# A hybrid decoder layer: the Mamba branch's TensorE instructions in a written order instead of the planner's

## The chip, the cores and the metric

The kernel runs on one core of one Trainium2 chip. The metric is device time in microseconds (us), the median of several executions; smaller is better. One core has TensorE (PE; its weight loads are shown as PEld), VectorE (DVE), ScalarE (ACT), GpSimd (POOL), the sync engine's queue (SP), which issues most transfers, and 16 DMA engines.

## The reference, cut to what matters

One layer on 512 tokens of width 1024, all in f32. A projection feeds an attention branch and a Mamba-2 branch; gates merge them, then come an output projection, a LayerNorm, a SwiGLU FFN and a second LayerNorm. The change touches the Mamba branch alone:

```
z, xbc, dt_raw = parts of x @ w_in
xbc = silu(causal_depthwise_conv(xbc, conv_w, conv_b))       # 4 taps along the tokens
xs, bm, cm = split(xbc, [2048, 2048 + 512])                  # 32 heads of 64; 4 groups of B and C, state 128
# chunks of 128 tokens, decay = exp(acum_t - acum_s) for s <= t
y_diag = (C B^T * decay) @ (x * dt)                          # within a chunk
h_next = h * exp(acum_last) + B^T @ (x * dt * decay_to_end)  # state, chunk to chunk
y = y_diag + exp(acum) * (C @ h_prev) + d_skip * xs
u = y * silu(z);  u = u * rsqrt(mean(u^2 per group) + eps) * norm_w
ssm_d = u @ w_proj_ssm
```

## The kernel before, in words

**A product.** `mm3` (L143) multiplies two operands that are each split in a rounded high part and a low rest: three matmuls (L144 to L146) of 128x128 weights by up to 512 columns. In this text one call of it is a step. Weights come by SP into `raw` tiles (4 buffers), ACT makes the high part (L102, `whi`) and DVE the low part (L103, `wlo`, 3 buffers each), both marked urgent.

**One group.** The branch has four groups `g` of eight heads. `group_bc` (L274) projects B and C of the group (8 steps each); `conv_evac` (L260) takes each result through the convolution: one ACT pass (L262), three DVE taps (L265), an ACT tanh (L268); `silu_to` (L272, DVE) ends it. B is then transposed on TensorE (four 128x128 transposes, L289), and C and B give four products (L295), which DVE masks into `cbm` (L296). `group_x` (L301) projects 256 columns of x per call (two blocks of 128, 16 steps in all), runs the same convolution on each block, transposes it (L311) and copies it to `xtok` (L312). `group_y` (L325) goes over four chunks: `xdt` (DVE, L338), two decay tiles `ab` loaded by SP from a table in HBM (L344), eight relu and two exp passes on ACT (L347, L348), two DVE products with `cbm` (L349); then TensorE makes eight products of 64 columns (L353, `py`), `C @ h_prev` (L362, `po`) and the state (L370, `pst`); POOL makes `dx` (L356) and `xw` (L368); DVE adds up `y` (L359 to L365) and the next state `hn` (L375, L376). `group_z` (L315) projects z (32 steps) and makes `gz`. `group_u` (L381) gates and normalises `y` (DVE L386, ACT L388, POOL L390, DVE L391) and transposes it (L395) into `uh` and `ul`. `group_proj` (L399) multiplies by the output weights (32 steps), and ACT or DVE adds the result to `sd` (L405, L407).

**PSUM.** There are four banks for the long products (`gps`) and four for everything short (`cps`). POOL's `xw`, `dx` have one buffer each, `xdt` two, `ab` six.

**The order.** The main loop is L647 to L666: for each group `group_y`, then the output projection of the group before, z, `group_u`, then B, C and x of the next group; at the end the q and k projections of the first heads and the last output projection. This text order is only a priority: a planner that builds the program takes, for each engine, the ready instruction of highest priority by its own estimate of time, and the result is a fixed order per engine. On the chip each engine runs its list in that order and waits where an operand is late. Where the kernel opens a manual region for an engine, the instructions of that engine stand in text order; `high_priority` marks instructions to be preferred.

The functions before the change:

Of the kernel before, what the change touches and what calls it, by code (L numbers as in the profile page):

```python
# [2 lines left out]

# [10 lines left out]
ALU = mybir.AluOpType  # L14
# [3 lines left out]
P = 128  # L18
T = 512
NT = T // P  # L20
# [6 lines left out]
NG = 4  # L27
# [14 lines left out]
def tile_hybrid_decoder_layer(  # L42
# [62 lines left out]
    def gps():  # L105
        return psum.tile([P, T], F32, name="gps", bufs=4)
# [43 lines left out]

    def gemm_ws(w, c0, nk, rhs, evac, alloc=gps, n=T, chunks=None):
# [9 lines left out]
        for b in range(2):  # L161
            evac(b, ps[b])

    def gemm_xs(w, c0, lhs, evac, before=None):


        ps = [gps() for _ in range(NT)]

# [10 lines left out]
        if before is None:  # L179
            for kc in range(KD // 2):  # L180
                hi, lo = split_w(fetch(kc), T)
                for tt in range(NT):
                    product(kc, tt, hi, lo)
            return
# [5 lines left out]
        with tc.manual_schedule(engines=ORDERED):  # L190
            for i in range(NT):
                before(i)
                for kc in range(len(chunks)):
                    product(kc, i, *chunks[kc])
                chunks.append(split_w(raw[i], T, urgent=False))
                if i == NT - 1:
                    small_weights()
                for tt in range(i + 1):
                    product(i, tt, *chunks[i])

    def down_chunk(w, kc, half, dst=None):
# [71 lines left out]

    def group_bc(g):  # L274
        st = {}
# [5 lines left out]
        for bi, nm in ((0, "bT"), (1, "cT")):  # L281
            v, th = conv_evac(16 + 4 * bi + g, gp[bi])
            st[nm] = slot(nm)
            silu_to(st[nm], v, th)
        bT, cT = st["bT"], st["cT"]
        btok = st["btok"] = slot("btok")
        ps = cps()
        for c in range(NT):
            nc.tensor.transpose(out=ps[:, c * P:(c + 1) * P], in_=bT[:, c * P:(c + 1) * P], identity=ident)  # L289
        nc.scalar.copy(out=btok, in_=ps)  # L290
        cbm = st["cbm"] = slot("cbm", (P, NT, P))
        ps = cps()
        for c in range(NT):
            cs = slice(c * P, (c + 1) * P)
            nc.tensor.matmul(out=ps[:, cs], lhsT=bT[:, cs], rhs=cT[:, cs], start=True, stop=True)  # L295
        nc.vector.tensor_tensor(out=cbm, in0=ps.rearrange("p (c l) -> p c l", c=NT),  # L296
                                in1=tri.rearrange("p (o l) -> p o l", o=1).broadcast_to([P, NT, P]), op=ALU.mult)
        st["xtok"] = big("xtok")
        return st

    def group_x(g, st, pair):  # L301
        xtok = st["xtok"]

        def evac(b, ps):
            j = 2 * pair + b
            v, th = conv_evac(4 * g + j, ps)
            xst = slot("xst")
            silu_to(xst, v, th)
            pt = cps()
            for c in range(NT):  # L310
                nc.tensor.transpose(out=pt[:, c * P:(c + 1) * P], in_=xst[:, c * P:(c + 1) * P], identity=ident)  # L311
            nc.scalar.copy(out=xtok[:, :, j * P:(j + 1) * P], in_=pt.rearrange("p (c f) -> p c f", c=NT))  # L312
        gemm_ws(w_in, C_X + g * 512 + pair * 256, KD, rhs_x, evac)

    def group_z(g, before=None):  # L315
        gz = big("gz")

        def evac(tt, ps):
            th = slot("th")
            nc.scalar.activation(out=th, in_=ps, func=AF.Tanh, scale=0.5)  # L320
            nc.vector.scalar_tensor_tensor(out=gz[:, tt, :], in0=th, scalar=1.0, in1=ps, op0=ALU.add, op1=ALU.mult)
        gemm_xs(w_in, C_Z + g * 512, lhs_x, evac, before)
        return gz

    def group_y(g, st):  # L325
        cT, btok, cbm, xtok = st["cT"], st["btok"], st["cbm"], st["xtok"]
# [5 lines left out]
        hprev = None  # L332
        ys = []
        for c in range(NT):
# [5 lines left out]
            for hf in range(2):  # L340
# [8 lines left out]
                nc.vector.tensor_tensor(out=m, in0=m, in1=cbm[:, c:c + 1, :].broadcast_to([P, 4, P]), op=ALU.mult)  # L349
                ms.append(m)  # L350
            py = cps()
# [3 lines left out]
            dx = slot("dx")  # L355
            nc.gpsimd.tensor_tensor(out=v8(dx), in0=v8(xc),  # L356
                                    in1=d_bc[:, h8].rearrange("p (h o) -> p h o", o=1).broadcast_to([P, 8, 64]), op=ALU.mult)
            y = slot("y")
            nc.vector.tensor_tensor(out=y, in0=py, in1=dx, op=ALU.add)  # L359
            if c > 0:  # L360
                po = cps()
                nc.tensor.matmul(out=po, lhsT=cT[:, cs], rhs=hprev, start=True, stop=True)  # L362
                yo = slot("yo")
                nc.vector.tensor_tensor(out=v8(yo), in0=v8(po), in1=bc8(ecum, c), op=ALU.mult)
                nc.vector.tensor_tensor(out=y, in0=y, in1=yo, op=ALU.add)  # L365
            if c < NT - 1:
                xw = slot("xw")
                nc.gpsimd.tensor_tensor(out=v8(xw), in0=v8(xc), in1=bc8(dtw, c), op=ALU.mult)  # L368
                pst = cps()
# [7 lines left out]
                hprev = hn  # L377
            ys.append(y)
        return ys

    def group_u(g, ys, gz):  # L381
        uh, ul = big("uh", 4, F32R), big("ul", 4, F32R)
        for c in range(NT):
            cs = slice(c * P, (c + 1) * P)
            y = ys[c]
# [5 lines left out]
            nc.vector.scalar_tensor_tensor(out=y, in0=y, scalar=ss[:, 1:2], in1=nw_bc[:, g * 512:(g + 1) * 512],  # L391
                                           op0=ALU.mult, op1=ALU.mult)
            pu = cps()
# [3 lines left out]
        return uh, ul  # L397

    def group_proj(g, u):  # L399
        uh, ul = u  # L400
        for pair in range(4):
            def evac(b, ps, pair=pair):
# [3 lines left out]
                else:  # L406
                    nc.vector.tensor_tensor(out=o, in0=ps, in1=o, op=ALU.add)  # L407
            gemm_ws(w_ps[g * 512:(g + 1) * 512], pair * 256, 4, lambda kt: (uh[:, kt, :], ul[:, kt, :]), evac)


    QK = (("v", "th", "bT", "cT"), ("btok", "cbm", "xst", "xdt"))

    def att_qk(hg, isq, qk):
        c0 = (C_Q if isq else C_K) + hg * 256
        sc = 0.125 if isq else 1.0

        def evac(b, ps):
            for par in range(2):
# [14 lines left out]
                qk[(isq, h)] = (t1, t2)  # L433
        gemm_ws(w_in, c0, KD, rhs_x, evac)

    def att_v(hg):
# [9 lines left out]
        gemm_xs(w_in, C_V + hg * 256, lhs_x, evac)  # L446
        return vt

# [192 lines left out]

    st = group_bc(0)
    for pair in range(2):
        group_x(0, st, pair)
    nw_bc = slot("nw", (P, 2048))
    nc.sync.dma_start(out=nw_bc, in_=ssm_norm_w.partition_broadcast(P))
    qk = {}  # L647
    u = None
    for g in range(NG):
        ys = group_y(g, st)  # L650
        if g == 0:
            st = group_bc(1)
            group_x(1, st, 0)
        else:
            group_proj(g - 1, u)
            gz = group_z(g)
        u = group_u(g, ys, gz)
        if g == 0:
            group_x(1, st, 1)
        elif g < NG - 1:  # L660
            st = group_bc(g + 1)
            for pair in range(2):
                group_x(g + 1, st, pair)
    att_qk(0, True, qk)
    att_qk(0, False, qk)
    group_proj(NG - 1, u)  # L666

# [7 lines left out]
    for hg in range(4):  # L675
        if hg > 0:
            att_qk(hg, True, qk)
            att_qk(hg, False, qk)
        if hg % 2 == 0:
            vts = att_v(hg)  # L680
        vt = vts[hg % 2]
# [413 lines left out]
```

## Time and profile before

| | us |
|---|---|
| median of 3 runs (lowest to highest) | 1146.16 (1146.07 to 1146.4) |
| profiled execution, its own time | 1149.0 |
| span of the profiled execution | 1147.3 |

The profile is of one execution, with times from the start of its span. Busy time of TensorE is a union of modelled matmul spans: a 512-column product is shown at 0.39 us though the next may start after 0.23 us. So here the starts of successive instructions are compared, not the spans. The stage that the change touches runs from about 44 to 438 us; attention, the output projection and the FFN follow.

### The profile page before, as it was taken

The numbers are of one execution on the slowest core, as the hardware profiler recorded it, in microseconds if no ns is written. First come the engines' busy times: TensorE is split into PE (matmuls) and PEld (weight loads), VectorE is DVE, ScalarE is ACT, GpSimd is POOL, SyncE is SP. The second block draws the span as 40 slices with busy tenths as digits, with TensorE's granted clock in tenths as the row PEclk, the third lists the DMA queues.
The fourth block names the chain that finished last, engine by engine and source line by source line (L and its number), as shares of the span: only waits on it lengthen the run. The fifth ranks groups of instructions, "written<-read, shape, count | busy, mean of one in ns | idle before, by whom it ended". The sixth has DMA issues, their size and how long they took to land.

```text
span 1147.3 us, 15795 instructions
## 1 busy us (share of the span) xinstructions
PE 1118.0 (97%) x6086; PEld 941.3 (82%) x6086; DVE 777.8 (68%) x1223; ACT 527.2 (46%) x912; POOL 134.1 (12%) x165
## 2 busy tenths in 40 slices
PE   7999999999999999999999999999999999999996
PEld 5887778778787788777777888888999999988885
DVE  2679974884786563889598534556997777767326
ACT  2476664454542432666465434214654554453210
POOL 3003130030122100221110000011111111100001
PEclk9999999999999999999999999999999999999998
DMA  6353233233232233211212245381778787465311
GB/s 195 110 169 127 75 112 101 82 111 101 83 94 58 89 92 96 70 57 56 77 53 56 76 127 183 108 204 59 199 184 204 183 195 164 91 231 174 102 55 74
DMA packets 116060, 134.20 MB, mean 117 GB/s; under 512 B 5669, under 2 KB 94481, under 8 KB 115857
## 3 DMA queue, kind: packets, MB, share of 16 engines
q1 hardware_dynamic: 98896, 111.75, 31.8%
q0 software_dynamic: 14640, 14.10, 7.7%
q10 hardware_dynamic: 2448, 7.34, 1.8%
q8 instruction: 48, 0.79, 0.3%
q14 instruction: 28, 0.22, 0.1%
HBM read 128.78 MB, written 4.26 MB: 116 GB/s over the span
## 4 chain that ended last, share of the span: by engine, by line
PE 44%; DVE 3%; issue 3%; DMA 2%; ACT 1%; POOL 0%; POOLq 0%; DVEq 0%; ACTq 0%
PE gps L145 9%; PE gps L144 9%; PE gps L146 9%; PE cps L145 5%; PE cps L146 5%; PE cps L144 4%; DMA rq<-in_w_ffn_up_dram 1%; PE cps L480 1%; PE cps L486 1%; DMA t_sd<-in_x_dram 0%; DVE xr L763 0%; PE cps L458 0%; DMA raw<-in_w_ffn_down_dram 0%; PE cps L459 0%; DVE wlo L103 0%
## 5 line engine op out<-in xcount | busy, mean ns | idle before, releaser
L103 DVE TENSOR_TENSOR wlo<-raw,whi 128x1024 fp32r<-128x1024 f32 x127 | 156.2, 1230 | 189.3 <-ACT whi L102 188.6
L102 ACT CAST whi<-raw 128x1024 fp32r<-128x1024 f32 x127 | 133.4, 1051 | 253.5 <-PE gps L145 101.9
L145 PE MATMUL gps<-xl,whi 128*128 128x512 f32 x456 | 181.2, 397 | 0.0
L144 PE MATMUL gps<-xh,whi 128*128 128x512 f32 x456 | 181.0, 397 | 0.0
L146 PE MATMUL gps<-xh,wlo 128*128 128x512 f32 x456 | 180.8, 396 | 0.0
L102 ACT CAST wh<-rq 128x1024 fp32r<-128x1024 f32 (+1 forms) x84 | 82.2, 980 | 101.7 <-PE cps L145 44.6
L103 DVE TENSOR_TENSOR wl<-rq,wh 128x1024 fp32r<-128x1024 f32 (+1 forms) x84 | 95.0, 1132 | 34.2 <-ACT wh L102 34.1
L144 PEld LDWEIGHTS gps<-xh,whi 128*128 128x128 f32 x456 | 85.9, 188 | 16.3 <-issue 0.2
L145 PEld LDWEIGHTS gps<-xl,whi 128*128 128x128 f32 x456 | 86.0, 189 | 16.1 <-issue 0.2
L146 PEld LDWEIGHTS gps<-xh,wlo 128*128 128x128 f32 x456 | 86.0, 189 | 15.4
L144 PE MATMUL gps<-whi,xh 128*128 128x512 f32 x192 | 76.1, 397 | 1.9 <-ACT whi L102 1.6
L145 PE MATMUL gps<-wlo,xh 128*128 128x512 f32 x192 | 75.8, 395 | 1.0 <-DVE wlo L103 1.0
L146 PE MATMUL gps<-whi,xl 128*128 128x512 f32 x192 | 75.8, 395 | 0.0
L265 DVE SCALAR_TENSOR_TENSOR t_v<-gps,cw,t_v 128x511 f32<-128x511 f32 (+2 forms) x72 | 53.4, 745 | 3.9 <-ACT t_v L262 3.1
L145 PE MATMUL gps<-t_ul,whi 128*128 128x512 f32 x128 | 51.1, 399 | 0.0
L146 PE MATMUL gps<-t_uh,wlo 128*128 128x512 f32 x128 | 51.0, 399 | 0.0
L144 PE MATMUL gps<-t_uh,whi 128*128 128x512 f32 x128 | 50.5, 394 | 0.0
L144 PEld LDWEIGHTS gps<-whi,xh 128*128 128x128 f32 x192 | 36.5, 190 | 10.7 <-ACT whi L102 2.0
L465 ACT ACTIVATE t_y<-t_y,sm 128x128 f32<-128x128 f32 (+1 forms) x64 | 35.7, 559 | 19.4 <-DVE sm L463 17.7
L347 ACT ACTIVATE t_ab<-t_ab,acum 128x128 f32<-128x128 f32 x128 | 41.6, 391 | 5.7 <-DMA t_ab<-ac_d 5.4
L821 POOL DMA_DIRECT2D rq<-in_w_ffn_gate_dram x12 | 15.5, 1294 | 245.7 <-ACT xh L723 159.0
L145 PEld LDWEIGHTS gps<-wlo,xh 128*128 128x128 f32 x192 | 36.5, 190 | 9.3 <-DVE wlo L103 1.9
(567 smaller groups left out, 2761.3 us busy)
## 6 DMA issues: line engine op xcount, KB each, us to landing
raw<-in_w_in_dram SPq DMA_DIRECT2D x80, 512.0 KB, 3.7
rq<-in_w_ffn_gate_dram SPq DMA_DIRECT2D x25, 512.0 KB, 5.8
rq<-in_w_ffn_up_dram SPq DMA_DIRECT2D x25, 512.0 KB, 5.9
raw<-in_w_ffn_down_dram SPq DMA_DIRECT2D x22, 512.0 KB, 4.0
t_ab<-ac_d SPq DMA_DIRECT2D x32, 256.0 KB, 3.3
raw<-in_w_proj_ssm_dram SPq DMA_DIRECT2D x16, 512.0 KB, 3.5
rq<-in_w_ffn_gate_dram POOLq DMA_DIRECT2D x10, 512.0 KB, 7.8
rq<-in_w_ffn_up_dram POOLq DMA_DIRECT2D x10, 512.0 KB, 6.4
```

The costliest lines, as they stand in the source:

```text
L102: nc.scalar.copy(out=hi, in_=src)
L103: nc.vector.tensor_tensor(out=lo, in0=src, in1=hi.bitcast(F32), op=ALU.subtract)
L144: nc.tensor.matmul(out=o, lhsT=l[0], rhs=r[0], start=start, stop=False, skip_group_check=skip)
L145: nc.tensor.matmul(out=o, lhsT=l[0], rhs=r[1], start=False, stop=False, skip_group_check=skip)
L146: nc.tensor.matmul(out=o, lhsT=l[1], rhs=r[0], start=False, stop=stop, skip_group_check=skip)
L265: nc.vector.scalar_tensor_tensor(out=v[:, sh:], in0=ps[:, 0:T - sh], scalar=cw[:, k, blk:blk + 1], in1=v[:, sh:], op0=ALU.mult, op1=ALU.add)
L347: nc.scalar.activation(out=m[:, r, :], in_=m[:, r, :], func=AF.Relu, scale=-1.0, bias=acum[:, c, h:h + 1])
L465: nc.scalar.activation(out=pt[:, 0:n], in_=pt[:, 0:n], func=AF.Exp, scale=-1.0, bias=sm[:, 2:3], accum_out=sm[:, 0:1])
L480: nc.tensor.transpose(out=ps[:, o:o + P], in_=pr[i][:, kb * P:(kb + 1) * P], identity=ident)
L486: nc.tensor.matmul(out=po[:, kb * P:], lhsT=vt[:, kb, hh, :], rhs=pT[kb][j], start=kb == 0 and j == 0, stop=kb == NT - 1 and j == 1)
L821: nc.gpsimd.dma_start(out=self.v(t), in_=self.q(*s_), accum_op=ALU.add)
```

## The change

For the whole branch TensorE gets a manual region: its instructions run in the order of the text. The functions become generators that yield after each step, and the main loop says how many steps stand between them. `fill(steps, n)` runs n steps; `later` holds transposes (and the C*B products) with a count of steps after which they are put in. The count is lowered right after the step that finished the source, so `[9, ...]` means 8 further steps, 8 means 7 and 10 means 9. `at(steps, ns, what)` runs the given numbers of steps and a piece of `what` after each. Results of the two blocks of one x pair are now evacuated when each block's last step is issued. The convolution, the copy to `xtok`, the whole of `y_steps` and `u_steps` are marked high priority. In a chunk of y the preparation (`xdt`, `ab`, `xw`, `dx`) is one piece and the TensorE products (`py`, `po`, `pst`) with what follows them another; `hn` comes ahead of `y`. Helpers `ws_steps`, `xs_steps`, `proj_steps` are the old loops with a yield after each `mm3`. No arithmetic, tile or transfer is added or removed. The core:

```diff
+    later = []
+
+    def fill(steps, n=10 ** 6):
+        for _ in range(n):
+            if next(steps, 0) == 0:
+                return
+            for e in later:
+                e[0] -= 1
+            while later and later[0][0] <= 0:
+                later.pop(0)[1]()
+
+    def bc_steps(g, st):
...
+                if kt == KD - 1:
+                    nm = ("bT", "cT")[bi]
+                    with tc.high_priority():
+                        v, th = conv_evac(16 + 4 * bi + g, gp[bi])
+                        st[nm] = slot(nm)
+                        silu_to(st[nm], v, th)
+                    later.append([9, (b_tok, c_b)[bi]])
+                yield 1
...
+    def x_steps(g, st, pair):
...
+            with tc.high_priority():
+                v, th = conv_evac(4 * g + j, ps)
+                xst = slot("xst")
+                silu_to(xst, v, th)
...
+            later.append([(8, 10)[b], to_tokens])
+        yield from ws_steps(w_in, C_X + g * 512 + pair * 256, KD, rhs_x, evac)
...
+    def y_steps(g, st, ys):
...
+            if c < NT - 1:
+                xw = slot("xw")
+                nc.gpsimd.tensor_tensor(out=v8(xw), in0=v8(xc), in1=bc8(dtw, c), op=ALU.mult)
+            dx = slot("dx")
...
+            yield 1
             py = cps()
...
+    def u_steps(g, ys, gz):
...
+        yield 1
+        for c in range(NT):
...
             pu = cps()
...
+            yield 1
...
+    def at(steps, ns, what):
+
+        for n in ns:
+            fill(steps, n)
+            with tc.high_priority():
+                next(what)
+
+    def bcx(g):
+        return chain(bc_steps(g, sts[g]), x_steps(g, sts[g], 0), x_steps(g, sts[g], 1))
+
+    with tc.manual_schedule(engines={mybir.EngineType.PE}):
+        fill(bcx(0))
+        nw_bc = slot("nw", (P, 2048))
+        nc.sync.dma_start(out=nw_bc, in_=ssm_norm_w.partition_broadcast(P))
+        for g in range(NG):
+            after = bcx(g + 1) if g < NG - 1 else chain(att_qk(0, True, qk), att_qk(0, False, qk))
+            ys = []
+            if g == 0:
+                fill(after, 11)
+                at(after, (0, 3, 0, 6, 0, 6, 0, 6), y_steps(g, sts[g], ys))
+                at(after, (0, 6, 3, 3, 3), u_steps(g, ys, gz))
+            else:
+                proj = proj_steps(g - 1, *u[0])
+                fill(proj, 11)
+                at(proj, (0, 4, 0, 6, 0, 6, 0, 5), y_steps(g, sts[g], ys))
+                fill(proj)
+                gz, steps = group_z(g)
+                fill(steps)
+                at(after, (0, 8, 3, 3, 3), u_steps(g, ys, gz))
+            fill(after)
+        fill(proj_steps(NG - 1, *u[0]))
```

## Rows read from the trace of the kernel before

**Rows 1.** The page, part 1: busy time of TensorE, its share, instructions.
```profile
PE 1118.0 (97%) x6086; PEld 941.3 (82%) x6086; DVE 777.8 (68%) x1223; ACT 527.2 (46%) x912; POOL 134.1 (12%) x165
```

**Rows 2.** Timeline, TensorE, ends of the stage (start us, us, instruction).
```profile
44.38 0.39 PE L144 MATMUL gps<-xh,whi 128*128 128x512 f32 x1
...
45.74 0.39 PE L144 MATMUL gps<-xh,whi 128*128 128x512 f32 x1
...
438.00 0.39 PE L144 MATMUL gps<-whi,xh 128*128 128x512 f32 x1
```

**Rows 3.** Timeline, TensorE, the u transposes of group 1.
```profile
196.57 0.39 PE L145 MATMUL gps<-xl,whi 128*128 128x512 f32 x1
...
204.21 0.63 PE L395 MATMUL cps<-ident,t_y 128*128 128x128 f32 x4 [0.73 <-DVE t_y L391]
...
204.90 0.39 PE L144 MATMUL gps<-xh,whi 128*128 128x512 f32 x1
```

**Rows 4.** Timeline, TensorE, state products of group 2.
```profile
243.63 0.40 PE L145 MATMUL gps<-t_ul,whi 128*128 128x512 f32 x1
...
246.15 1.12 PE L370 MATMUL cps<-t_xw,t_btok 128*128 128x512 f32 x2 [0.29 <-POOL t_xw L368]
247.12 1.89 PE L353 MATMUL cps<-t_xdt,t_ab 128*128 128x64 f32 x16
248.84 1.08 PE L362 MATMUL cps<-t_hn,t_cT 128*128 128x512 f32 x2
249.76 1.03 PE L370 MATMUL cps<-t_xw,t_btok 128*128 128x512 f32 x2
...
256.23 1.10 PE L353 MATMUL cps<-t_xdt,t_ab 128*128 128x64 f32 x8 [0.67 <-DVE t_ab L349]
...
260.60 0.39 PE L146 MATMUL gps<-t_uh,wlo 128*128 128x512 f32 x1
```

**Rows 5.** Timeline, TensorE, C*B products of group 1.
```profile
117.47 0.39 PE L144 MATMUL gps<-xh,whi 128*128 128x512 f32 x1
119.25 1.16 PE L295 MATMUL cps<-t_cT,t_bT 128*128 128x128 f32 x8 [1.39 <-DVE ss L389]
```

**Rows 6.** Timeline, all engines, convolution of an x block, group 2.
```profile
219.66 0.78 ACT L262 ACTIVATE t_v<-gps,vec,cw 128x512 f32<-128x512 f32 x1 [2.93 <-PE gps L146]
...
221.14 0.68 DVE L349 TENSOR_TENSOR t_ab<-t_ab,t_cbm 128x512 f32<-128x512 f32 x1
...
223.00 0.74 DVE L265 SCALAR_TENSOR_TENSOR t_v<-gps,cw,t_v 128x509 f32<-128x509 f32 x1
...
223.12 0.77 ACT L262 ACTIVATE t_v<-gps,vec,cw 128x512 f32<-128x512 f32 x1
...
223.66 1.22 DVE L103 TENSOR_TENSOR wlo<-raw,whi 128x1024 fp32r<-128x1024 f32 x1
...
223.84 0.63 ACT L268 ACTIVATE t_th<-t_v 128x512 f32<-128x512 f32 x1
...
224.79 0.69 DVE L272 SCALAR_TENSOR_TENSOR t_xst<-t_th,t_v 128x512 f32<-128x512 f32 x1
...
225.59 0.39 PE L144 MATMUL gps<-xh,whi 128*128 128x512 f32 x1
225.82 0.60 PE L311 MATMUL cps<-ident,t_xst 128*128 128x128 f32 x4
...
226.49 0.40 PE L146 MATMUL gps<-xh,wlo 128*128 128x512 f32 x1
...
231.14 0.63 PE L311 MATMUL cps<-ident,t_xst 128*128 128x128 f32 x4
```

**Rows 7.** One line, VectorE: count, duration in ns min/median/max.
```profile
L338 DVE TENSOR_TENSOR t_xdt<-t_xtok,dt x16: 677/693/1534, 94.2 to 348.4; 128x512 f32<-128x512 f32 x16
```

**Rows 8.** Windows of one group (projections and convolutions, then state products): length, busy by engine.
```profile
195.40:243.80 48.40, 47.07 (x225) 37.41 (x224) 39.70 (x59) 22.85 (x36) 3.74 (x5) 1.00 0.27 77
243.80:260.60 16.80, 15.85 (x89) 11.62 (x89) 14.75 (x19) 10.21 (x28) 9.08 (x7) 1.00 0.46 141
```

More of the change, by code (lines that the diff above doesn't have):

```diff
@@ L2 @@
 from contextlib import ExitStack
+from itertools import chain
 import concourse.bass as bass
@@ L149, in ws_chunk, with drain, gemm_ws, ws_steps @@
         return load_w(w[half * 512:(half + 1) * 512, c0:c0 + 256], 4, 256, dst)
-    def gemm_ws(w, c0, nk, rhs, evac, alloc=gps, n=T, chunks=None):
+    def drain(steps):
+        for _ in steps:
+            pass
+    def gemm_ws(*args):
+        drain(ws_steps(*args))
+    def ws_steps(w, c0, nk, rhs, evac, alloc=gps, n=T, chunks=None):
         ps = [alloc()[:, 0:n] for _ in range(2)]
@@ L160, in gemm_ws @@
                     mm3(ps[b], (hi[k][:, bs], lo[k][:, bs]), rhs(kt), kt == 0, kt == nk - 1)
-        for b in range(2):
-            evac(b, ps[b])
+                    if half == nk // 4 - 1 and k == 3:
+                        evac(b, ps[b])
+                    yield
     def gemm_xs(w, c0, lhs, evac, before=None):
-        ps = [gps() for _ in range(NT)]
+        ps = [] if before is None else [gps() for _ in range(NT)]
         def fetch(kc):
@@ L179, in gemm_xs @@
         if before is None:
[L180 to L183, printed above, removed]
+            for _ in xs_steps(w, c0, lhs, evac):
+                pass
             return
@@ L272, in silu_to, with b_tok, c_b @@
         nc.vector.scalar_tensor_tensor(out=o, in0=th, scalar=1.0, in1=v, op0=ALU.add, op1=ALU.mult)
-    def group_bc(g):
-        st = {}
-        gp = [gps() for _ in range(2)]
+    later = []
[8 more added lines that the diff above has]
+    def bc_steps(g, st):
+        gp = [gps() for _ in range(2)]
+        def b_tok():
+            btok = st["btok"] = slot("btok")
+            ps = cps()
+            for c in range(NT):
+                nc.tensor.transpose(out=ps[:, c * P:(c + 1) * P], in_=st["bT"][:, c * P:(c + 1) * P], identity=ident)
+            nc.scalar.copy(out=btok, in_=ps)
+        def c_b():
+            cbm = st["cbm"] = slot("cbm", (P, NT, P))
+            ps = cps()
+            for c in range(NT):
+                cs = slice(c * P, (c + 1) * P)
+                nc.tensor.matmul(out=ps[:, cs], lhsT=st["bT"][:, cs], rhs=st["cT"][:, cs], start=True, stop=True)
+            nc.vector.tensor_tensor(out=cbm, in0=ps.rearrange("p (c l) -> p c l", c=NT),
+                                    in1=tri.rearrange("p (o l) -> p o l", o=1).broadcast_to([P, NT, P]), op=ALU.mult)
         for bi, c0 in ((0, C_B + g * P), (1, C_C + g * P)):
@@ L280, in group_bc @@
                 mm3(gp[bi], (hi[kt], lo[kt]), rhs_x(kt), kt == 0, kt == KD - 1)
[L281 to L301, printed above, removed]
+                if kt == KD - 1:
+                    nm = ("bT", "cT")[bi]
[6 more added lines that the diff above has]
+    def x_steps(g, st, pair):
+        if pair == 0:
+            st["xtok"] = big("xtok")
         xtok = st["xtok"]
@@ L305, in evac, with to_tokens @@
             j = 2 * pair + b
[L306 to L313, printed above, removed]
+            with tc.high_priority():
+                v, th = conv_evac(4 * g + j, ps)
+                xst = slot("xst")
+                silu_to(xst, v, th)
+            def to_tokens():
+                pt = cps()
+                for c in range(NT):
+                    nc.tensor.transpose(out=pt[:, c * P:(c + 1) * P], in_=xst[:, c * P:(c + 1) * P], identity=ident)
+                with tc.high_priority():
+                    nc.scalar.copy(out=xtok[:, :, j * P:(j + 1) * P], in_=pt.rearrange("p (c f) -> p c f", c=NT))
+            later.append([(8, 10)[b], to_tokens])
+        yield from ws_steps(w_in, C_X + g * 512 + pair * 256, KD, rhs_x, evac)
     def group_z(g, before=None):
@@ L392, in group_u @@
                                            op0=ALU.mult, op1=ALU.mult)
+        yield 1
+        for c in range(NT):
+            cs = slice(c * P, (c + 1) * P)
+            y = ys[c]
             pu = cps()
@@ L640, in tile_hybrid_decoder_layer @@
     nc.scalar.activation(out=cuT[96:112], in_=cuT[32:48].bitcast(F32), func=AF.Copy, scale=-1.0)
[L642 to L646, printed above, removed]
-    qk = {}
[L648 to L666, printed above, removed]
+    sts = [{} for _ in range(NG)]
+    qk = {}
+    u = [None]
+    def at(steps, ns, what):
+        for n in ns:
+            fill(steps, n)
+            with tc.high_priority():
+                next(what)
[22 more added lines that the diff above has]
+        fill(proj_steps(NG - 1, *u[0]))
+    assert not later
     oslots = [slot("hn", (P, T), F32R) for _ in range(2)]
@@ L676, in tile_hybrid_decoder_layer @@
         if hg > 0:
[L677 to L678 removed]
+            drain(att_qk(hg, True, qk))
+            drain(att_qk(hg, False, qk))
         if hg % 2 == 0:
[L680 removed]
+            vts, steps = att_v(hg)
+            drain(steps)
         vt = vts[hg % 2]
```

48 lines of the change are left out of this document (26 added, 22 removed).

## The prediction, made before the change was timed

> **What bounds the kernel now.** I read the page first: TensorE is shown busy for 97% of the span [rows 1]. That hides small waits, because a 512-column product is drawn 0.39 us long while starts follow each other at 0.227 us (six starts in 1.36 us [rows 2]). So I compared starts. The stage goes from the first product of B to the first of v: 393.6 us [rows 2]. Its 1344 long products (448 steps) take 304.8 us at 0.2268. Four transposes put between two products cost 0.45 us (0.90 us from 225.59 to 226.49, less two products [rows 6]); a group has nine such quads, 4.1 us, and C*B is twice a quad, 0.9. A chunk's state products cost 1.72 for `py`, 0.92 for `po`, and, taken alike, 0.87 for `pst` [rows 4]: 12.2 us per group. Four groups make 68.8 us, and the short products of the entry, which stay, some 4.5. Sum 378.1. So **15.5 us of the stage is TensorE waiting or switching**. That, and no more, is there to be won; work on other engines counts only where TensorE waits for it. The granted clock is 1.00 in the windows read [rows 8].
>
> Where the 15.5 us lie, by starts:
> - The u transposes. From 196.57 to 204.90 stand 20 products and four quads: 8.33 - 4.54 - 1.80 = 2.0 us lost, with DVE's last norm step as releaser [rows 3]. Groups 2 and 3 repeat it, group 0 loses nothing: 5.8 us.
> - The state products. From 243.63 to 260.60 are 13 products and group 2's four chunks: 16.97 - 2.95 - 12.2 = 1.8 us, waits for `xw` and for the decay product of DVE [rows 4]. The others by the same sum lose 0.7, 1.5 and 1.8: 5.8 us.
> - C*B of group 1: 1.78 us from the product before instead of 0.23, 1.6 us lost [rows 5].
> - The remaining 2.3 us are about 0.05 us at each of some fifty switches.
>
> **The change, part by part.** A step is three products, 0.68 us.
>
> (a) *u transposes 8 steps behind z, then every 3.* The first has 5.4 us, the last 17 steps or 11.6 us. After z's last step come an ACT tanh, three DVE passes of about 0.7 us (as `L272` [rows 6]), the square and POOL's power: about 5 us for the last chunk, far under 11.6. I take the wait as gone: **-5.8**. If DVE is late by one low split (1.22 [rows 6]) it still holds; bounds -5.8 to -4.
>
> (b) *State products by chunk, 4 to 6 steps after the preparation.* `xw` now starts with the preparation, 2.7 us or more ahead of `py`; its wait goes. Moved ahead with it on POOL is `dx`, on DVE `xdt` and two decay products, on ACT ten passes, on SP two `ab` loads, which stand before weight loads; three raw buffers ahead cover those. If that cover went, a late weight chunk would stop all of TensorE. `dx` of the next chunk waits for `y` of this one (one buffer), and the `xw` after it queues behind it; its reader is 6 steps and a `py` away. DVE was busy 14.75 of 16.80 us in this stretch [rows 8]; the same work is now spread over about 27 us of products and steps, so I leave 0.5 us per group of waiting, 2.0, where the bounds are 0 and today's 5.8: **-3.8**. Chunks that stood back to back are parted: two more switches per group, **+0.5**.
>
> (c) *C*B 8 steps behind C*: the wait of group 1 goes, since state products now stand in the lead: **-1.6**.
>
> (d) *x transposes 7 and 9 steps behind their block.* This is the new risk: in the old list the transposes stand where the planner thought xst ready. Now a transpose whose xst is late holds every projection behind it, and with them the release of weight buffers and so ACT's and DVE's splits. The first block has 7 steps, 4.76 us. Its chain without disturbance is 0.16 (drain) + 0.78 + three taps of 0.74 + 0.63 + 0.69 [rows 6] = 4.5, and five hand-overs of about 0.1 (from the last tap's end, 223.74, to the tanh, 223.84 [rows 6]): 4.95 with rounding. So it is at least 0.2 late. As it ran, it took 6.16 us from ACT's start to the transposes, 6.3 from the source, with two decay products and a low split put in by the planner [rows 6]: 1.6 late. The urgent mark lets the chain go first where both are ready, but pauses between dependent passes are still filled, so I take one foreign pass in place of three, 5.45 us: 0.7 late. Six of the eight first blocks pay it (in group 1 state products or u quads stand in the lead): **+4.2**, bounds 1.2 and 9.6. The second block has 9 steps, a quad and that wait, 7.3 us; it took 8.0, from ACT's start at 223.12 to the transposes at 231.14 [rows 6], with as many foreign passes. With fewer it is in time: 0, at worst 0.9 in each of six.
>
> (e) *B's transposes 8 steps behind.* In groups 2 and 3 the lead is 5.44 and three u quads, 6.8 us; the chain of 4.95 meets two or three low splits of u (0.7 each): 0.8 late, twice; in group 0, with the entry's DVE work beside it, 0.5. **+2.1**, bounds 0 and 5. Evacuations of projections and z are moved by a step or two with all banks free: nothing, for the next user of a bank comes four steps later; uncovered it would be 0.7 per pair.
>
> Sum: -5.8 - 3.8 + 0.5 - 1.6 + 4.2 + 2.1 = **-4.4 us**. TensorE is the bound before and after the stage, so what it gains moves the end one for one. The sum is against the span of 1147.3 (the profiled execution itself took 1149.0); as a difference I apply it to the median of 1146.16: **1141.8**. ACT, DVE and POOL are still ordered by the planner, so the stages behind may also shift by a microsecond or two either way.
>
> **Rivals.**
> 1. *The leads suffice.* (d) and (e) cost nothing and (b) goes to zero: -13.2 + 0.5, 1133.5. For it: DVE is busy 39.7 of 48.4 us in the stretch of convolutions [rows 8], so there is room. Against: 4.76 is under even the undisturbed chain.
> 2. *POOL holds DVE.* `xdt` takes 0.69 us as a rule and up to 1.53 [rows 7], the long ones beside a POOL pass. `xw` and `dx` now start together, next to `xdt` and the decay products. If one collision of 0.84 per chunk falls into the lead of the products, and half of those sixteen are not covered, (b) leaves 6.8 us in place of 2.0, and the sum is about +0.4: no change, 1146.5. Against it: many of these collisions are there already. The Trainium skill, "SBUF — State Buffer", section "Who interferes with whom", says that a DVE pass with two SBUF inputs and a GpSimd pass that reads SBUF cannot share, and that the later one blocks for the whole of the other; the two levels of [rows 7] agree with that rule, and by it this case comes out.
> 3. *The convolution chain outgrows its lead: slower.* DVE has 0.82 of the stretch filled [rows 8], and a chain that waits at each pause for a low split (1.22) is 7.6 us instead of 5.45. Then first blocks are 2.8 us late, six times 17 us, the sum +8: 1154. It decides at 6.2 us of chain (no gain) and 6.6 (measurably slower). For it: 8.0 us was measured for a second block [rows 6]. Against: a late transpose gives DVE the same time to catch up.
> 4. *The order stays in effect the same*, as the planner had put transposes just in time already, and waits that go here return at the next hand-over: no change.
>
> **How the numbers follow.** About 0.2% (2.3 us) can be told from no change. Forecast (1137 to 1143.9): 0.44. Rival 1 (1132 to 1137): 0.16. Rivals 2 and 4 (1143.9 to 1148.5): 0.12 and 0.09. Rival 3 (over 1148.5): 0.19. So faster 0.60, same 0.21, slower 0.19. The range from 1133 to 1150 leaves out some 0.03 below and 0.13 above; the likeliest case alone, with the bounds of (d), spans 1137 to 1146.
>
> **What would show it.** Right: `L395` without waits, state products with no idle for `xw`, and 0.5 to 1 us of idle before first-block `L311` for `L272`. The stage from B to v should be about 389 us long. Wrong: no idle at `L311` (then 1134), idle over 1.5 us there, idle at `L353` in most chunks, or long products waiting for `whi` or `wlo`, which would mean that the splits are late.

## The result, and the profile after

The changed kernel takes **1166.24 us** (median of 4 runs, 1162.0 to 1166.81) where the kernel before takes 1146.28 (4 runs, 1146.07 to 1147.38): ratio 1.0159, 95% interval 1.0145 to 1.0174. It is slower by 20 us; the prediction said 1141.8 and ended its range at 1150. The profiled execution took 1166.81 us. Its span is 1165.1 us, 17.8 above that of before. Medians and ratios leave out one slow execution, the fourth of no_mark, which took 2261.78 us. The page of after (parts 1 and 2), the first line against [rows 1]:

```profile
PE 1121.5 (96%) x6086; PEld 947.6 (81%) x6086; DVE 778.9 (67%) x1223; ACT 528.5 (45%) x912; POOL 125.6 (11%) x165
...
PEclk9989999999999999999999999999999999999999
```

The work is the same; the clock row has one slice at 8 near the start. The ends of the stage in the timeline of after (first product of B, first product of v; start us, us, engine, line) answer to [rows 2]:

```profile
43.93 0.39 PE L145 MATMUL gps<-xh,whi 128*128 128x512 f32 x1
...
455.59 0.39 PE L145 MATMUL gps<-whi,xh 128*128 128x512 f32 x1
```

The stage has grown from 393.62 to 411.66 us, by 18.04. What follows it took 709.26 us before and 709.5 after, so all of the loss is in this stage. What TensorE waits for there, in the view of waits of after (total us, times, longest; the five largest):

```profile
PE cps L353 <- DVE t_xst L292: 13.2, 8, 2.3
PE cps L659 <- DVE t_y L655: 5.2, 1, 5.2
PE cps L313 <- DVE t_bT L292: 3.0, 3, 1.3
PE cps L449 <- DVE ss L439: 0.5, 1, 0.5
PE gps L146 <- DVE t_ul L104: 0.5, 1, 0.5
```

The first four are written positions in which the operand was late: x's transposes (L353; L311 before), an entry product (L659; L606 before), B's transposes (L313), u's (L449). In the last a product waits for the low split of u. State products (L406, L413) and C*B (L321) are not in the list. By starts, with the prices of the prediction (0.2268 a product, 0.45 a quad, and so on), the time lost per kind is:

| | before | predicted change | after |
|---|---|---|---|
| u transposes and their splits | 5.8 | -5.8 | 1.6, all in group 0 |
| state products | 5.8 | -3.8 | 0.0 |
| C*B | 1.6 | -1.6 | 0.0 |
| x transposes, first blocks | 0.0 | +4.2 | 15.9 (2.40, 1.62, 3.50, 0.66, then twice 2.17 and 1.69) |
| x transposes, second blocks | 0.0 | 0 | 0.0 |
| B's transposes, groups 1 to 3 | 0.0 | +1.6 | 3.6 (0.57, 1.54, 1.54) |
| group 0: B's transposes and the entry | about 0 | +0.5 | 10.3 |

13.2 went and 31.4 came: 18.2, against 18.04 measured. The 3.50 is counted to 141.4 us; the lower clock that holds after it until about 142.6 adds 0.6. The small switches (2.3 us before) are not in the table.

**What went as intended.** A u quad of group 1 and the first chunk of group 2 in the timeline of after:

```profile
216.98 0.39 PE L147 MATMUL gps<-xh,wlo 128*128 128x512 f32 x1
217.21 0.60 PE L449 MATMUL cps<-ident,t_y 128*128 128x128 f32 x4
...
217.88 0.39 PE L146 MATMUL gps<-xl,whi 128*128 128x512 f32 x1
...
265.15 1.89 PE L406 MATMUL cps<-t_xdt,t_ab 128*128 128x64 f32 x16
266.88 1.08 PE L413 MATMUL cps<-t_xw,t_btok 128*128 128x512 f32 x2
```

From 216.98 to 217.88 stand a quad and two products, 0.90 us, the price without a wait; [rows 3] had 0.73 of idle there. `py` takes its 1.73 and `pst` follows without a pause, where [rows 4] show waits for `xw` and the decay product.

**Where the x transposes lose.** The first x block of group 2 in the timeline of all engines of after, to be set beside [rows 6]:

```profile
235.36 0.39 PE L147 MATMUL gps<-xh,wlo 128*128 128x512 f32 x1
...
235.79 0.78 ACT L282 ACTIVATE t_v<-gps,vec,cw 128x512 f32<-128x512 f32 x1 [2.81 <-PE gps L147]
...
236.69 0.74 DVE L285 SCALAR_TENSOR_TENSOR t_v<-gps,cw,t_v 128x511 f32<-128x511 f32 x1
...
237.35 0.68 DVE L395 TENSOR_TENSOR t_ab<-t_ab,t_cbm 128x512 f32<-128x512 f32 x1
...
237.94 0.74 DVE L285 SCALAR_TENSOR_TENSOR t_v<-gps,cw,t_v 128x510 f32<-128x510 f32 x1
...
238.60 0.68 DVE L395 TENSOR_TENSOR t_ab<-t_ab,t_cbm 128x512 f32<-128x512 f32 x1
...
239.20 0.74 DVE L285 SCALAR_TENSOR_TENSOR t_v<-gps,cw,t_v 128x509 f32<-128x509 f32 x1
...
239.86 1.22 DVE L104 TENSOR_TENSOR wlo<-raw,whi 128x1024 fp32r<-128x1024 f32 x1
...
240.04 0.63 ACT L288 ACTIVATE t_th<-t_v 128x512 f32<-128x512 f32 x1
...
240.99 0.74 DVE L285 SCALAR_TENSOR_TENSOR t_v<-gps,cw,t_v 128x511 f32<-128x511 f32 x1
241.65 0.68 DVE L292 SCALAR_TENSOR_TENSOR t_xst<-t_th,t_v 128x512 f32<-128x512 f32 x1
...
242.48 0.63 PE L353 MATMUL cps<-ident,t_xst 128*128 128x128 f32 x4 [1.97 <-DVE t_xst L292]
```

and the same stretch in the view of windows (us, then busy time and count of PE, PEld, DVE, ACT, POOL, granted clock, DMA share, GB/s):

```profile
235.40:242.50 7.10, 5.13 (x24) 3.96 (x22) 7.10 (x12) 3.14 (x4) 0.00 (x0) 1.00 0.27 76
```

Every pause of the chain (between two taps, during the tanh) holds a pass of something else: a decay product, another, a low split of weights, a tap of the *second* block. That makes four foreign passes, and VectorE is busy 7.10 of 7.10 us. The source's last product starts at 235.36 and the next one at 235.59. From there to the transposes at 242.48 the chain takes 6.9 us; the lead is 4.76. The 2.1 us between them are lost, and 1.97 of them are shown as the idle ahead of L353.

**The entry.** TensorE in the timeline of after, with idle and releaser in brackets, and two windows behind the wait:

```profile
55.17 0.39 PE L147 MATMUL gps<-xh,wlo 128*128 128x512 f32 x1
60.72 0.77 PE L659 MATMUL cps<-t_y,tri 128*128 128x128 f32 x2 [5.16 <-DVE t_y L655]
...
66.38 1.04 PE L683 MATMUL cps<-ident,acum 128*32 128x128 f32 x4 [0.38 <-DVE acum L668]
...
68.24 1.06 PE L313 MATMUL cps<-ident,t_bT 128*128 128x128 f32 x4
68.95 0.77 PE L145 MATMUL gps<-xh,whi 128*128 128x512 f32 x1
```

```profile
61.00:63.00 2.00, 2.00 (x11) 2.00 (x11) 0.50 (x1) 0.00 (x0) 0.00 (x0) 0.50 0.04 11
...
71.00:73.00 2.00, 2.00 (x11) 1.62 (x10) 0.00 (x0) 0.22 (x1) 0.00 (x0) 1.00 0.26 97
```

B's transposes of group 0 stand at step 16, and ahead of them the entry's short products (cumulative sums of the decay), which need L655 of VectorE. TensorE has nothing else that it may run: idle for 5.16 us. Then the granted clock is 0.50, the lower level, until about 71 us, and what runs takes about twice its time (the first long products follow each other at 0.43 to 0.57 us in place of 0.23). 10.3 us are lost: 5.5 of idle, the rest by the clock. The trace of before had the clue, in rows that the prediction does not use (VectorE, then TensorE):

```profile
58.29 0.69 DVE L272 SCALAR_TENSOR_TENSOR t_bT<-t_th,t_v 128x512 f32<-128x512 f32 x1
...
64.38 0.60 PE L636 MATMUL cps<-ident,t_y 128*16 128x128 f32 x4
64.82 0.60 PE L289 MATMUL cps<-ident,t_bT 128*128 128x128 f32 x4
```

B was ready at 58.98, yet its transposes stood at 64.82, right behind the entry's last short product. They were held by that order, not by B; only projections of x, which the planner let pass in front, kept TensorE at work meanwhile. The written order puts those projections behind B's transposes.

### The profile page after: what moved, and what is told of

Same layout as the page of the kernel before. It is cut to its first block, busy times and chain, and to the rows that moved or that the text cites. A ratio compares the mean times of both kernels' runs of the same rounds, so it can differ in the third digit from the quotient of the medians.

```text
span 1165.1 us, 15791 instructions
## 1 busy us (share of the span) xinstructions
PE 1121.5 (96%) x6086; PEld 947.6 (81%) x6086; DVE 778.9 (67%) x1223; ACT 528.5 (45%) x912; POOL 125.6 (11%) x165
## 4 chain that ended last, share of the span: by engine, by line
PE 43%; DVE 3%; issue 3%; DMA 2%; ACT 1%; POOL 0%; POOLq 0%; DVEq 0%; ACTq 0%
PE gps L146 9%; PE gps L145 9%; PE gps L147 9%; PE cps L146 5%; PE cps L147 4%; PE cps L145 4%; DMA rq<-in_w_ffn_up_dram 1%; PE cps L533 1%; PE cps L539 1%; DMA t_sd<-in_x_dram 1%; DVE xr L828 0%; PE cps L511 0%; DMA raw<-in_w_ffn_down_dram 0%; PE cps L512 0%; DVE wlo L104 0%
## 5 line engine op out<-in xcount | busy, mean ns | idle before, releaser
L145 PE MATMUL gps<-xh,whi 128*128 128x512 f32 x456 | 185.7, 407 | 0.0
L145 PE MATMUL gps<-t_uh,whi 128*128 128x512 f32 x128 | 54.3, 424 | 0.0
L393 ACT ACTIVATE t_ab<-t_ab,acum 128x128 f32<-128x128 f32 x128 | 41.1, 390 | 18.2 <-DMA t_ab<-ac_d 13.0
L147 PEld LDWEIGHTS gps<-whi,xl 128*128 128x128 f32 x192 | 36.3, 189 | 8.7 <-DVE xl L104 1.3
```

Source lines behind the costliest of these rows:

```text
L145: nc.tensor.matmul(out=o, lhsT=l[0], rhs=r[0], start=start, stop=False, skip_group_check=skip)
L147: nc.tensor.matmul(out=o, lhsT=l[1], rhs=r[0], start=False, stop=stop, skip_group_check=skip)
L393: nc.scalar.activation(out=m[:, r, :], in_=m[:, r, :], func=AF.Relu, scale=-1.0, bias=acum[:, c, h:h + 1])
```

## The experiments

Each is the changed kernel with the edit shown; the arithmetic stays. Theory A: VectorE stretches the convolution chain beyond its counted lead, and the lead decides. Theory C: group 0's B transposes pull the entry's short products, and with them the wait for VectorE, ahead of x's steps. Further letters in the expectations are rivals, told where they occur. "Lost" is always by starts, as in the table.

**x_lead_11: both blocks of x 11 steps behind.**

```diff
-            later.append([(8, 10)[b], to_tokens])
+            later.append([(12, 12)[b], to_tokens])
```

> Both blocks of an x pair get their transposes 11 steps (7.5 us) behind the block instead of 7 and 9. Theory A (the convolution chain takes about 6.9 us with the passes that the planner puts into its pauses, and what the lead lacks of it is lost): the waits before first-block transposes, 15.9 us in sum, go, second blocks stay without, time about 1166.2 - 15.9 = 1150. Rival B (VectorE is full in this stretch, so the lateness only moves to the next hand-over): a third of it at most comes back, 1160 or more.

Measured: 1161.4 us, 1.0133 of before (1.0112 to 1.0154). The waits of TensorE in the stage:

```profile
PE cps L449 <- DVE t_y L441: 4.9, 1, 4.9
PE cps L353 <- DVE t_xst L292: 4.0, 5, 0.8
```

First blocks lose nothing now, second blocks about 1.0 each in five places. So A holds for the places: the 15.9 of the first blocks are gone. But the sum missed, and the total is that of rival B (1160 or more): 5.0 came back at second blocks, and u's transposes of group 0 lose 7.8 in one place (4.89 idle, then the lower clock until about 153.8 us). VectorE, which TensorE no longer lets catch up at x, is late for u instead.

**entry_late: group 0's B transposes and C*B behind 24 and 16 steps.**

```diff
-                    later.append([9, (b_tok, c_b)[bi]])
+                    later.append([(25, 17)[bi] if g == 0 else 9, (b_tok, c_b)[bi]])
```

> In group 0 alone the transposes of B and the C*B products stand behind step 32 instead of steps 16 and 24, so that 16 more steps are free to run while the short products of the entry wait. Theory C (the transposes of B of group 0 stand behind the entry's products, and all steps of x behind them, so TensorE idles 5.2 us and the next 10 us run at the lower clock): the 10.3 us lost around 61 us go, granted clock 1.00 there, time about 1156. Rival D (the urgent mark on the convolutions delays the entry's chain on VectorE, and that is the loss): the entry still ends as late, under 3 us come back, 1163 or more.

Measured: 1155.42, 1.008 (1.0059 to 1.0101), 10.8 below after. The entry in the timeline and the windows:

```profile
61.24 0.38 PE L659 MATMUL cps<-t_y,tri 128*128 128x128 f32 x2
```

```profile
61.20:66.20 5.00, 5.00 (x38) 4.43 (x38) 2.57 (x6) 2.31 (x5) 0.00 (x0) 1.00 0.30 88
```

No idle, clock 1.00, loss 0.06 in place of 10.3: C holds. Rival D is right about VectorE, but that is not the loss: L655 ends at 60.57 us in after, its counterpart L602 at 59.17 before, with three urgent taps of C put ahead of it; here it ends later still, at 60.98, and nothing is lost. The edit also puts B's transposes and C*B into the lead of the first x block, which waits 0.25 us in place of 2.18. The short products L659 to L665 need 2.60 us here (61.24 to 63.84) and 5.28 in after (60.72 to 66.38, less the idle of 0.38).

**btok_gps: group 0's B transposes in a bank of the long products.** This asks why they stood behind the entry at all: if it was the allocation order of the short banks, another bank frees them at the same count of steps.

```diff
-            ps = cps()
+            ps = gps() if g == 0 else cps()
```

> In group 0 alone the transposes of B take a bank of the long products' four instead of the short products' four; their place, 8 steps behind B, stays. Theory C1 (they stand behind the entry's products because those take the short banks first): they run right behind step 16, at about 57 us, the steps of x go on, at most 2 us are lost there, time 1157 to 1158. Rival C2 (the planner takes the entry's products first because they stand earlier in the text): nothing changes, 1166.

Measured: 1161.64, 1.0138 (1.012 to 1.0156).

```profile
56.66 0.66 PE L313 MATMUL gps<-ident,t_bT 128*128 128x128 f32 x4 [0.80 <-DVE t_bT L292]
...
61.29 0.38 PE L659 MATMUL cps<-t_y,tri 128*128 128x128 f32 x2
...
78.94 1.09 PE L353 MATMUL cps<-ident,t_xst 128*128 128x128 f32 x4 [4.12 <-DVE t_xst L292]
```

The transposes run at 56.66, x's steps follow, and the entry's products come at 61.29 without a wait. So it was the bank. The price came back in part, though, and the time missed C1's 1157 to 1158: with TensorE no longer stopped at the entry, the first x block is 4.12 us late (5.7 lost, at the lower clock again).

**no_mark: no urgent mark on the convolution, TensorE's order unchanged.** The rival E to A: it is the mark, not the lead, that sets how many foreign passes stand in the chain.

```diff
-                    with tc.high_priority():
+                    with ExitStack():
...
-            with tc.high_priority():
+            with ExitStack():
```

> The convolution chains lose their urgent mark; TensorE's order stays. Theory A (the mark orders only what is ready at the same time and does not keep other passes out of the pauses of the chain): first-block waits stay within 0.5 us each, time 1163 to 1170. Rival E (the mark holds the chain short, without it every chain grows by a pass or more): 14 chains times 0.7 us or more, over 1174.

Measured: 1186.14 (median of three runs, 1183.98 to 1186.52), 1.0346 (1.0324 to 1.0369), the range of E. VectorE ahead of the first x block of group 0, timeline:

```profile
82.33 1.90 DVE L395 TENSOR_TENSOR t_ab<-t_ab,t_cbm 128x512 f32<-128x512 f32 x3 [2.22 <-ACT t_ab L394]
84.15 4.03 DVE L285 SCALAR_TENSOR_TENSOR t_v<-gps,cw,t_v 128x511 f32<-128x511 f32 x6
88.27 1.35 DVE L292 SCALAR_TENSOR_TENSOR t_xst<-t_th,t_v 128x512 f32<-128x512 f32 x2
```

Decay products that still wait for ACT (2.22 us) stand ahead of the whole convolution, whose transposes lose 11.4, with the lower clock that follows. Groups 0 and 1 lose 9.1 each in two more places, groups 2 and 3 4.7 and 3.1 at the first block where after loses 2.17. At the entry TensorE waits 3.31 us in place of 5.16. I had expected little difference; the mark is worth 20 us. It orders ready work, but after shows that it does not keep pauses empty.

**all_leads: entry late, x 11 steps, B of groups 1 to 3 also 11.**

```diff
+                    later.append([(25, 17)[bi] if g == 0 else (12, 9)[bi], (b_tok, c_b)[bi]])
...
+            later.append([(12, 12)[b], to_tokens])
```

> Three leads together: both x blocks 11 steps, B's transposes 11 steps in groups 1 to 3, and in group 0 B's transposes and C*B behind step 32. Theory A (each loss is what the lead lacks, and they add): from 1166.2 the entry's 10.5, the first blocks' 10.8 (second blocks keep 1.0 each) and B's 2.6 go, the wait of 6 before the u transposes of group 0 comes as in the run with 11 steps alone: about 1149. Rival G (waits taken away return elsewhere, since VectorE had used them to catch up): 1154 or more.

Measured: 1149.79, 1.0019 (1.0007 to 1.003), what A expected. B's transposes lose nothing; what is left is 6.7 at u of group 0, 2.3 at one x block of it, and 1.0 at each second block of groups 2 and 3.

**leads_13: also two more steps for second blocks and for y.**

```diff
-            later.append([(8, 10)[b], to_tokens])
+            later.append([(12, 14)[b], to_tokens])
...
-                fill(after, 11)
+                fill(after, 13)
...
-                at(after, (0, 6, 3, 3, 3), u_steps(g, ys, gz))
+                at(after, (0, 5, 3, 3, 3), u_steps(g, ys, gz))
...
-                fill(proj, 11)
-                at(proj, (0, 4, 0, 6, 0, 6, 0, 5), y_steps(g, sts[g], ys))
+                fill(proj, 13)
+                at(proj, (0, 4, 0, 5, 0, 5, 0, 5), y_steps(g, sts[g], ys))
```

> As the run with the three leads, but second x blocks 13 steps behind, and the state products of each group two steps later, with the spacing after them one step tighter. Theory A: the second blocks' last 5 us go, 1144 to 1145, about level with the kernel before; what is left is the wait in group 0. Rival H (the decay products and xdt now come late, since they start two steps later and stand closer): idle before the state products, 1149 or more.

Measured: 1148.87, 1.0018 (1.0008 to 1.0027), above A's 1144 to 1145. Rival H's idle before the state products did not come. x is settled (0.5 of waiting in all) and groups 2 and 3 lose 0.5 each, at C*B. Yet group 0's stretch takes it all back:

```profile
PE cps L449 <- DVE t_y L441: 5.5, 1, 5.5
PE gps L145 <- ACT t_uh L103: 1.6, 1, 1.6
```

**u0_later: y of group 0 spread over 8 steps a chunk, u(0) under z of group 1.** The rival here, L: lateness only moves on to the next written position.

```diff
-                at(after, (0, 3, 0, 6, 0, 6, 0, 6), y_steps(g, sts[g], ys))
-                at(after, (0, 6, 3, 3, 3), u_steps(g, ys, gz))
+                at(after, (0, 3, 0, 8, 0, 8, 0, 8), y_steps(g, sts[g], ys))
...
+                at(steps, (4, 4, 4, 4), us)
+                both = chain(steps, proj_steps(g - 1, *u[0]))
+                at(both, (0, 4, 0, 8, 0, 8, 0, 8), y_steps(g, sts[g], ys))
```

> As the run with 13 steps, and besides group 0's state products stand 8 steps apart, its u transposes come under z of group 1, and z of group 1 comes ahead of the output projection of group 0, so that the norm of group 0 no longer has to fit beside the convolutions of group 1. Theory K (there VectorE has more work than TensorE, about 52 against 49 us, and the 6 us are that excess): the wait before the u transposes of group 0 goes, 1138 to 1140, better than before. Rival L (the excess only moves to the state products of group 1): 1144 or more.

Measured: 1146.49, 0.9995 (0.9983 to 1.0007). No wait at u any more; in its place:

```profile
107.52 2.08 PE L321 MATMUL cps<-t_cT,t_bT 128*128 128x128 f32 x8 [2.88 <-DVE t_cT L292]
109.38 3.51 PE L406 MATMUL cps<-t_xdt,t_ab 128*128 128x64 f32 x16
```

C*B waits 2.88 us, and `py` takes 3.51 in place of 1.89 at the lower clock: 7.9 lost there, and 2.1 in a product that waits for the taps to free its bank. L holds.

**m_pool: the changed kernel with the 32 decay products on GpSimd.** If A is right that foreign passes stretch the chain, two of four go; the rival M says that POOL's passes hold VectorE's.

```diff
-                nc.vector.tensor_tensor(out=m, in0=m, in1=cbm[:, c:c + 1, :].broadcast_to([P, 4, P]), op=ALU.mult)
+                nc.gpsimd.tensor_tensor(out=m, in0=m, in1=cbm[:, c:c + 1, :].broadcast_to([P, 4, P]), op=ALU.mult)
```

> The changed kernel with the decay products (32 passes) on GpSimd instead of VectorE, leads as they were. Theory A (two foreign decay products in the first chain of groups 2 and 3 make it late): their first-block waits fall from 2.0 to about 0.7 us, 1160 to 1163 in sum. Rival M (GpSimd's passes of about 1.4 us hold VectorE's two-input passes and themselves come late): state products wait, 1168 or more.

Measured: 1169.06, 1.0191 (1.0174 to 1.0208). The same x block of group 2, VectorE and then POOL:

```profile
236.14 2.31 DVE L285 SCALAR_TENSOR_TENSOR t_v<-gps,cw,t_v 128x511 f32<-128x511 f32 x3 [1.76 <-ACT t_v L282]
238.90 1.69 DVE L104 TENSOR_TENSOR wlo<-raw,whi 128x1024 fp32r<-128x1024 f32 x1 [0.45 <-ACT whi L103]
240.51 0.74 DVE L285 SCALAR_TENSOR_TENSOR t_v<-gps,cw,t_v 128x511 f32<-128x511 f32 x1
241.17 1.09 DVE L292 SCALAR_TENSOR_TENSOR t_xst<-t_th,t_v 128x512 f32<-128x512 f32 x1
...
234.45 8.95 POOL L395 TENSOR_TENSOR t_ab<-t_ab,t_cbm 128x512 f32<-128x512 f32 x6 [11.49 <-DVE t_cbm L322]
```

The three taps now run back to back: the pauses between them are free. But the pause at the tanh still holds the low split and a tap of the second block, and beside POOL's passes the split takes 1.69 in place of 1.22 and the last pass 1.09 in place of 0.68. The transposes wait 2.36 in place of 1.97. The taps, which read a PSUM bank, keep their 0.74. The Trainium skill, "SBUF — State Buffer", section "Who interferes with whom", says that a VectorE pass with two SBUF inputs contends with a GpSimd pass that reads SBUF, and that the port pair which they share is an exclusive lock; these lengths agree that such passes grow and the taps do not. So A's expectation missed, and M's total came out, though not through the state products, which wait for nothing. As the decay products stretch other passes from POOL, the run does not show what two foreign passes fewer alone would do.

**from_group_1: the planner's order for group 0's stretch, the written one with long leads from the first projection on.**

```diff
+    fill(bcx(0))
...
+    drain(y_steps(0, sts[0], ys))
+    after = bcx(1)
+    fill(after, 32)
+    drain(u_steps(0, ys, gz))
+    fill(after)
     with tc.manual_schedule(engines={mybir.EngineType.PE}):
...
-        for g in range(NG):
+        for g in range(1, NG):
```

with transposes right behind their sources and no marks in `group_bc` and `group_x` of groups 0 and 1.

> The planner orders TensorE through group 0's stretch as before the change (sources and transposes in the old text order, no marks on the convolutions of groups 0 and 1); the written order starts with the output projection of group 0, with the long leads (B 11 steps, x 11 and 13). Theory K (the written order is good where VectorE has room, groups 1 to 3, and bad only beside the convolutions of group 1 and at the entry): of the 15.5 us of the old stage the u transposes' 5.8 and the state products' 5.1 in groups 1 to 3 go, 0.9 comes at C*B: 1136 to 1138, better than both. Rival N (what the planner leaves late at the seam stops the written order there): 1142 or more.

Measured: 1144.34 against 1147.37, 0.9971 (0.996 to 0.9983): faster than before, by less than K expected, and in the range of N. About 6 us are still lost at 136 us, where the planner's part meets the written one (2.9 of it a wait of an x transpose), which is N's mechanism.

**leads_by_group: entry late, the change's own leads for groups 0 and 1, those of leads_13 for groups 2 and 3.**

```diff
+                    later.append([(25, 17)[bi] if g == 0 else 9 if g == 1 else (12, 9)[bi], (b_tok, c_b)[bi]])
...
+            later.append([((8, 10) if g < 2 else (12, 14))[b], to_tokens])
...
+                fill(proj, 13 if g > 1 else 11)
+                at(proj, (0, 4, 0, 5, 0, 5, 0, 5) if g > 1 else (0, 4, 0, 6, 0, 6, 0, 5), y_steps(g, sts[g], ys))
```

> The changed kernel with the entry's correction of group 0, its own leads in groups 0 and 1 and the long ones (B 11, x 11 and 13) in groups 2 and 3. Theory A (each wait is what its own lead lacks): 1155.4 of the run with the entry's correction alone less 7.7 for the four first blocks and 2.1 for B, 1145 to 1146, and the 8 us of group 0's stretch stay. Rival G: over 1149.

Measured: 1144.2 against 1147.37, 0.9974 (0.9964 to 0.9983), about a microsecond below what A expected; it beats both kernels. The stage has 388.87 us. Its largest wait:

```profile
PE cps L353 <- DVE t_xst L292: 5.0, 4, 2.6
```

All of these lie between 78 and 145 us; groups 2 and 3, whose first blocks lost 7.7 us in after, lose 0.48 each, and nothing new comes up in their place.

**leads_by_group2: longer leads also for x of group 0 and B of group 1.** The theory K to be tried: from about 96 to 145 us VectorE itself is full, so leads cannot help there.

```diff
+            later.append([((12, 12), (8, 10), (12, 14), (12, 14))[g][b], to_tokens])
```

> As the run with leads by group, but both x blocks of group 0 get 11 steps and B of group 1 gets 11. Theory A: the 2.4 us before the first blocks of group 0 and the 0.6 before B of group 1 go, 1141 to 1142. Theory K (VectorE is the bound from about 100 to 145 us, so what is not waited for there at one place is waited for at another): under 1.5 us come back, 1143 or more.

Measured: 1144.39 against 1146.87, 0.9973 (0.9963 to 0.9984): no gain over leads_by_group. The losses moved (2.13 at 93.6; 4.3 at 126.9, with the lower clock that follows) and about kept their sum. The same 49 us in the windows of leads_by_group, then of before:

```profile
96.00:145.00 49.00, 44.53 (x233) 34.70 (x232) 46.44 (x69) 32.60 (x72) 8.93 (x10) 1.00 0.33 98
96.00:145.00 49.00, 47.32 (x244) 37.64 (x244) 44.91 (x68) 35.22 (x76) 11.24 (x10) 1.00 0.31 97
```

VectorE is busy 46.4 of 49 us in the best version, and longer leads won nothing there; so far K holds. It does not hold that VectorE alone sets the time of this stretch: in the planner's order of before TensorE is busy 47.3 us of it and VectorE 44.9. By starts, before loses 3.0 us between 78 and 145 us and leads_by_group 8.6. So another order loses less here, though the branch has the same work; what in it does so was not tried.

## Why the prediction was wrong, point by point

- **(a) u transposes: right for groups 1 to 3**, where the 5.8 are gone. Group 0, which I had at nothing, now loses 1.6; the net of 4.2 lies within the bounds.
- **(b) state products: right in sign, better in size.** Nothing waits in after; the 2.0 that I left for waiting was too careful. Rival 2 did not occur: `xdt` takes 683, 694 and 1551 ns (least, median, most), nearly the values of [rows 7], and TensorE does not wait for it. Its mechanism is real, as m_pool shows, but this change set it off nowhere on TensorE's path.
- **(c) C*B: right.**
- **(d) x transposes: this step failed in its size, 15.9 in place of 4.2, above its upper bound of 9.6.** The sentence that failed is "I take one foreign pass in place of three". The chain has five hand-overs, and an urgent mark does not hold a pause open: while a tap is in flight its successor isn't ready, and the planner puts in what is. Four passes went in, more than before, and 5.45 us became 6.9. The mark was not useless (no_mark: 20 us worse), but it chose the order of ready passes only. I had also let state products and u quads cover group 1; its blocks lose 3.50 and 0.66. x_lead_11 shows that the lead decides where the wait stands: with 11 steps, and nothing else changed, the first blocks wait for nothing. In groups 2 and 3 that is the whole cause, for there the loss goes with longer leads and does not come back (leads_by_group). In groups 0 and 1 most of it came back at other places, for VectorE is late there as a whole.
- **(e) B's transposes: groups 1 to 3 mis-sized** (3.6 in place of 1.6), for the same reason; with 11 steps the loss is gone in all_leads. **Group 0 was a mechanism that I missed**: 0.5 predicted, 10.3 measured. I costed only how late B itself would be, and a wait only by its idle time: about half of the 10.3 is the lower clock behind the wait. What stood ahead of it in the same four banks I did not ask, though the 5.84 us between B's end at 58.98 and its transposes at 64.82 lay open in the trace. entry_late and btok_gps show it.
- **Sum and chances.** "Idle over 1.5 us there" at the first-block transposes was named as the sign of a wrong forecast, and that is what came: four of the eight waits are 1.97 to 2.26 us, two more 1.49. Rival 3, given 0.19, was the mechanism for the larger half, though with four mixed passes and not a low split at each pause; 6.9 us was measured, above the 6.6 from which it expected a loss. Rival 1 fell with the first waits. Rival 4's return of waits at the next hand-over is what x_lead_11 and u0_later show in groups 0 and 1, but the sum was no standstill. Rival 3's price, 2.8 for six blocks less the gains, gave 1154; eight blocks of about 2 and an entry that it did not contain gave 1166.
- **TensorE's gains and losses move the end one for one**: right (709.3 and 709.5 us behind the stage).

Left open: which order of group 0's stretch would be best, why the planner's loses less there than every written one, and how much of VectorE's load there could be moved elsewhere without meeting POOL. The clock's share varies from run to run: entry_late's profiled execution, with granted clock 0.997, took 1152.66, its others, with 0.993 to 0.995, up to 1156.44.

## What to carry to other kernels

A written order on one engine is only as good as the counted leads, and a lead must be measured against the chain as a *filled* engine runs it: as a first estimate from this one chain (four foreign passes at five hand-overs) count about one foreign pass for every hand-over, since the priority mark ordered ready work and kept no gap open. Before something is fixed behind n steps, look at what stood directly ahead of it in the old list and in its buffers, not only at when its operand was ready: an old list in which work flows past a late instruction hides a dependency that a written order exposes. Where an engine off the critical path was nearly full over a stretch, longer leads only moved the wait on. Compare such a stretch with the old list before calling it full: here the planner's order lost less in it.

## What the runs showed of the hardware that I had not expected

- After TensorE had stood idle for 5.16 us (after), 4.89 (x_lead_11) or 4.12 (btok_gps), the windows that follow show a granted clock of 0.50, so that such a wait cost more than its idle time (10.3 for 5.5; 7.8 for 4.9; 5.7 for 4.1). Shorter waits went either way. After 2.26 us in after (x of group 1, 139.19) and 2.36 in m_pool (x of group 2) the granted clock is 0.50 as well, and 4.1 and 4.2 us are lost. After 2.59 in leads_by_group and 1.97 in after's groups 2 and 3 it stays at 1.00, and the loss is the idle and about 0.2 for the switch. I had priced waits by their idle time alone.
- In m_pool VectorE passes with both inputs in SBUF grew beside GpSimd, short ones too: 0.68 to 1.09, 1.22 to 1.69, and `xdt`'s median from 694 to 1201 ns.
